# A two-layer encoder: the last 512 tokens split 384 and 128 instead of 256 and 256, a shorter final root, four final norms on GpSimd, and another order of the first loads

## The chip, the cores and the metric

One core of a Trainium2 chip runs the whole kernel. The metric is the device time of one execution in microseconds, the median of several. The engines are named as in the profile: PE is TensorE (PEld its weight loads), DVE is VectorE, ACT is ScalarE, POOL is GpSimd, SP is SyncE, which here only issues transfers. A small q (SPq, ACTq) stands for an engine's sequencer, which issues DMAs.

## The reference, cut to what matters

The input `x` is 1024 tokens by 1024 features in float32; two layers follow each other, and a last norm stands at the end. What the change touches is the first product of layer 0 and the end of layer 1:

```python
for l in range(DEPTH):                       # DEPTH = 2
    h = _rmsnorm(x, g_mix[l])                # x * rsqrt(mean(x*x) + 1e-6) * g
    p = h @ w_in[l]
    ...                                      # latent attention and a convolution branch
    x = x + y
    h2 = _rmsnorm(x, g_ffn[l])
    z = _dwconv(h2 @ w_up[l], w_dw_ffn[l], b_dw_ffn[l])
    zg, zv = jnp.split(z, 2, axis=-1)
    x = x + (jax.nn.silu(zg) * zv) @ w_down[l]
return _rmsnorm(x, g_final)
```

## The kernel before, in words

The residual stream lies transposed: eight blocks of 128 features (partitions) by 1024 tokens (columns). A product with float32 accuracy is made of three products of rounded operands: upper weight with upper x, upper with lower, lower with upper. So each operand is split in two on ACT (the rounded upper part) and DVE (the rest), and each product of a 128 x 128 weight tile with 512 tokens is three TensorE instructions.

**The start** is `run` (L367) and `first_sections` (L385). Three sections of the first weight matrix (g0, a0, g1) are multiplied with the eight blocks of x. The norm's gain is folded into x (`upper_x`, `lower_x`), and its root is applied later, to the products; for it ACT squares the blocks and DVE adds them up in `xss`. The work is written out by hand: the loads in program order on SP (one, of g0's first 256 columns, on ACT), then the casts and subtractions, then the products. TensorE begins with eleven products of ones (`WARM`), then six pairs on block 0 with g0 and a0, then `order` (L472): blocks 1 to 7 with all three sections, and g1 on blocks 0 and 1. The first 256 columns of a weight section are the tiles of blocks 0 and 1, the rest those of blocks 2 to 7. After block 5 the sums in `xss` are turned on TensorE (`turned`, 8 transposes), which needs the last addition.

**The end** is `down_steps` (L1196), the down projection, written as a list of steps: `steps[n]` holds the products of step n, and `put(n, rank, f)` places other work behind step n in order of rank. That fixes the order of the instructions on each engine; each still waits for its own data. In layer 1 the last six weight tiles (`TAIL_STEPS`) of the last product group are multiplied in eight steps: first for the token range `ENDS[0]`, feature blocks m = 0 to 3, then for `ENDS[1]`, 18 products a step. A finished piece is added to x on DVE (`evict_end`), squared on ACT, and the square is added to the sums on DVE (`gather_end`), but that of m = 3, which TensorE sums directly. `end_root` sums over features on TensorE (`column_sums`: an f32 product with a column of ones per 128 tokens, two passes each) and takes the inverse root on DVE (`roots`: nine small instructions). For `ENDS[0]` the root is spread back over features by transposes (`end_spread`), and `norm_apply` multiplies the blocks, on DVE out of PSUM, or on POOL for the blocks of `TAIL_POOL` with a copy that ACT makes, after ACT has multiplied the gain in (`end_scale`). SP stores each block, in the order of the program. For `ENDS[1]` the blocks, with their gains in, are turned on TensorE (`end_turn`), so that tokens lie on partitions and the root is one number per partition; `after` (L1358) multiplies by it, half on DVE, half on ACT, and stores to `out_tail`.

Of the kernel before, what the change touches and what calls it, by code (L numbers as in the profile page):

```python
# [16 lines left out]
T = 1024  # L17
# [14 lines left out]
EPS = 1e-6  # L32
RSQRT = 0x5F3759DF
GROUP = 2
SCALE = 1.0 / float(np.sqrt(NOPE + ROPE))
# [52 lines left out]
TAIL_STEPS = 6  # L88
ENDS = (slice(512, 768), slice(768, T))
LEAD_HEADS = 3  # L90
# [3 lines left out]
BANK_SET = {1: 0, 6: 0, 7: 0, 4: 0, 5: 1, 3: 1, 2: 1}  # L94
TAIL_POOL = (5, 7)
WARM = 11
# [20 lines left out]
class Encoder:  # L117
# [105 lines left out]

    def sumsq(self, acc, x, first, name, n=T, tag=None):
        nc = self.nc
        if first:
            nc.scalar.activation(out=acc, in_=x, func=AF.Square)
        else:
            sq = (self.tmp(tag, name) if tag else self.blk(name))[:, 0:n]
            nc.scalar.activation(out=sq, in_=x, func=AF.Square)  # L230
            nc.vector.tensor_tensor(out=acc, in0=acc, in1=sq, op=ALU.add)

    def column_sums(self, acc, name, parts, bank, more=None):
        nc = self.nc
        ps = bank(name + "p")
        blocks = [b for s in parts for b in range(s.start, s.stop, 128)]
        for i, b in enumerate(blocks):
            nc.tensor.matmul(ps[:, i:i + 1], acc[:, b:b + 128], self.ones[:, 0:1], start=more is None or i == 0, stop=more is None)
        for i in range(len(blocks) if more is not None else 0):
            nc.tensor.matmul(ps[:, i:i + 1], more[:, i * 128:(i + 1) * 128], self.ones[:, 0:1], start=False, stop=i == len(blocks) - 1)  # L240
        return ps[:, 0:len(blocks)]
# [10 lines left out]
    def roots(self, ps, w, n, name):  # L252
# [19 lines left out]
        return y  # L272

    def rsqrt_cols(self, acc, n, name, parts, bank, more=None, turned=False):
        w = sum(s.stop - s.start for s in parts) // 128
        if turned:
            return self.roots(self.turned(acc, name, parts, bank), w, n, name)
        return self.roots(self.column_sums(acc, name, parts, bank, more), w, n, name)

# [87 lines left out]
    def run(self):  # L367
        nc, a = self.nc, self.a
        self.par = [self.cp.tile([128, NPAR], F32, name="par0")]
        nc.sync.dma_start(out=self.par[0][:, 0:8], in_=a["par"][0][:, 0:8])  # L370
        self.x0 = self.blk("x0")
        nc.sync.dma_start(out=self.x0[:, HALVES[0]], in_=a["x"][0][:, HALVES[0]])
        self.ones = self.cp.tile([128, 128], F32, name="ones")
        nc.vector.memset(self.ones, 1.0)
        self.ones_r = self.cp.tile([128, 128], F32R, name="ones_r")
        self.xm = [self.dp.tile([8, 128, T], F32, name=f"x_mix{l}") for l in range(DEPTH)]
        self.actd = [self.dp.tile([NF, 128, T], F32, name=f"act{l}") for l in range(DEPTH)]
        self.wsd = [self.dp.tile([NF // 2, 2, 128, T], F32, name=f"ws{l}") for l in range(DEPTH)]
        self.xd = [a["x"], self.dp.tile([8, 128, T], F32, name="x_mid")]
        carry = None  # L380
        with self.tc.manual_schedule(engines=set(MANUAL)):
            for l in range(DEPTH):
                carry = self.layer(l, carry)

    def first_sections(self, l, supply):  # L385
# [3 lines left out]
             for n in names]  # L389
        x, acc = [self.x0] + [self.blk(f"x{k}") for k in range(1, 8)], self.blk(f"xss{l}")  # L390
        hl = [[self.tmp("m", f"xs{l}_{k}{i}", F32R) if k >= 4 else self.blk(f"xs{l}_{k}{i}", F32R) for i in "hl"]
# [24 lines left out]
        def upper_x(k, c=every):  # L416
            nc.scalar.activation(out=hl[k][0][:, c], in_=x[k][:, c], func=AF.Copy, scale=par[:, P_GMIX + k:P_GMIX + k + 1])

        def lower_x(k, c=every):
            nc.vector.scalar_tensor_tensor(out=hl[k][1][:, c], in0=x[k][:, c], scalar=par[:, P_GMIX + k:P_GMIX + k + 1],  # L420
                                           in1=hl[k][0][:, c].bitcast(F32), op0=ALU.mult, op1=ALU.subtract)

        def square(k):
            self.sumsq(acc, x[k], k == 0, f"xsq{l}_{k}")
# [11 lines left out]
        nc.sync.dma_start(out=self.par[0][:, 8:NPAR], in_=self.a["par"][0][:, 8:NPAR])  # L436
        self.par += [self.const(f"par{i}", [128, NPAR], self.a["par"][i]) for i in range(1, DEPTH)]
# [17 lines left out]
        lower(1, rest)  # L455
        lower_x(2)
        square(0)
        upper_x(3)
# [737 lines left out]
    def down_steps(self, l, steps, put):  # L1196
# [77 lines left out]
        def evict_end(c, m):  # L1274
            xm = x[4 + m][:, ENDS[c]]
            sub(xm, ps[BANK_SET[4], m][:, cols[c]], xm, ALU.add)

            sq[c, m] = self.blk(f"xsq{l}_e{c}{m}")[:, 0:256]
            nc.scalar.activation(out=sq[c, m], in_=xm, func=AF.Square)
# [46 lines left out]
        for m in range(4):  # L1326
# [3 lines left out]
            for c in range(2):  # L1330
                n = n5 + 4 * c + m
                put(n + 1 - c, 1 + c, lambda c=c, m=m: evict_end(c, m))
                if m < 3:
                    put(n + 1, 2.5 if c else 2.6, lambda c=c, m=m: gather_end(c, m))
        for f in range(NF):
# [22 lines left out]
        def after():  # L1358
            if not last:
                nxt["x"] = x  # L1360
                return nxt
            out = [self.blk(f"end{b}") for b in range(2)]
            for b in range(2):
                for i, cs in enumerate(HALVES):
                    o, ps, y = out[b][:, cs], turns[b, i], nxt["d"][:, b:b + 1]
                    if i == 0:
                        nc.vector.tensor_scalar(out=o, in0=ps, scalar1=y, scalar2=None, op0=ALU.mult)
                    else:
                        nc.scalar.activation(out=o, in_=ps, func=AF.Copy, scale=y)
                    (nc.scalar if b and i else nc.sync).dma_start(out=a["out_tail"][b][:, cs], in_=o)  # L1370

        def end_turn(i):
            for b, tag in enumerate(("d7", "d6") if i == 0 else ("d2", "d3")):
                turns[b, i] = self.pp.tile([128, 512], F32, name=f"end{i}{b}", tag=tag, bufs=1)
                at = ENDS[1].start + b * 128
                for k in range(4):
                    nc.tensor.transpose(turns[b, i][:, k * 128:(k + 1) * 128], x[4 * i + k][:, at:at + 128], self.ident)

# [5 lines left out]
        def end_root(c):  # L1384
            self.norm_root(l + 1, nxt, 1, spare, ENDS[c], sq.pop((c, 3)))

# [9 lines left out]
        if last:  # L1396
            put(n5 + 5, 0.5, lambda: end_root(0))
            put(n5 + 4, 3.5, lambda: end_scale(0))
            put(n5 + 6, 1.8, lambda: end_spread(0, (2, 5, 7, 0, 1)))
            put(n5 + 7, 3, lambda: end_apply(0, (3, 4, 6)))  # L1400
            put(n5 + 5, 3.5, lambda: end_scale(1, range(4)))
            for m in range(4):
                put(n5 + 4 + m, 2.55, lambda m=m: end_scale(1, (4 + m,)))
            put(n5 + 7, 3.9, lambda: end_turn(0))
            put(n5 + 7, 4, lambda: end_root(1))
            put(n5 + 7, 4.1, lambda: end_turn(1))
        return after

    def norm_sums(self, l, x, nxt, c, ks, cs=None):
# [3 lines left out]
        for k in ks:  # L1413
            self.sumsq(nxt["acc"][:, cs], x[k][:, cs], k == 0, f"xsq{l}_{cs.start}{k}", cs.stop - cs.start, None if c else "m")

# [399 lines left out]
def _layout(inputs):  # L1815
# [31 lines left out]
    def taps(w, k):  # L1847
# [4 lines left out]
         vec(f["g_conv_ln"]), vec(f["b_conv_ln"]), vec(f["g_ffn"]), taps(f["w_dw_ffn"], 3),  # L1852
         vec(f["b_dw_ffn"])], axis=2))
    out["g_final"] = c(f["g_final"].reshape(8, 128).T)
    out["ident"] = np.eye(128, dtype=np.float32)
# [22 lines left out]
```

## Time and profile before

| | us |
|---|---|
| median of 3 runs | 2251.2 (2250.36 to 2254.52) |
| the profiled execution | 2251.68 |
| its span | 2249.9 |
| PE busy in the span | 2225.7 |
| DVE, ACT, POOL busy | 1687.8, 1235.2, 693.4 |

The page gives busy time and its share of the span for each engine; PE is a pipelined engine, and its being busy does not say how much it computes. All durations below are from this one execution, so sums are made against 2251.68 and its span.

### The profile page before, as it was taken

To read this page: it belongs to the slowest core of one execution; us is meant where nothing else is said; L and a number is where in the kernel's file an instruction comes from. 1 tells how busy PE (TensorE), PEld (TensorE's weight loads), DVE (VectorE), ACT (ScalarE), POOL (GpSimd) and SP (SyncE) were. 2 spreads that over 40 slices of the span, in tenths; PEclk is the share of its full clock that TensorE was granted. 3 is DMA by queue.
4 is the path that set the end of the run, shared out by engine and by line. 5 is a ranking of instruction groups with operands and counts; after the bars stand their busy time and mean duration, and the time that the engine had idled before them with its cause. 6 is when DMAs were issued, how large, how long until landed. Compare 5 with 4: busy or idle time off the path is not lost. (4 is left out here: it accounts for less than half of the span.)

```text
span 2249.9 us, 34444 instructions
## 1 busy us (share of the span) xinstructions
PE 2225.7 (99%) x12746; PEld 1790.3 (80%) x12746; DVE 1687.8 (75%) x2241; ACT 1235.2 (55%) x1885; POOL 693.4 (31%) x781
## 2 busy tenths in 40 slices
PE   9999999999999999999999999999999999999998
PEld 7887666888888888888888876668888888888887
DVE  6998898669777776776559778876787777768765
ACT  5444777447655555544523457774475555555444
POOL 1221586332333332002412226652323333320032
PEclk9999999999999999999999999999999999999999
DMA  6889998765999998935968999986669999988356
GB/s 186 162 171 279 193 216 184 206 174 125 227 269 304 276 300 206 331 106 144 207 133 167 201 265 198 196 197 177 159 155 232 291 291 278 292 211 300 102 127 168
DMA packets 201160, 472.85 MB, mean 210 GB/s; under 512 B 28352, under 2 KB 35616, under 8 KB 200992
## 3 DMA queue, kind: packets, MB, share of 16 engines
q0 software_dynamic: 102704, 220.91, 48.9%
q1 hardware_dynamic: 98000, 249.35, 33.6%
q8 instruction: 100, 1.64, 0.3%
q14 instruction: 68, 0.56, 0.1%
q10 hardware_dynamic: 288, 0.39, 0.0%
HBM read 306.14 MB, written 80.40 MB: 172 GB/s over the span
## 5 line engine op out<-in xcount | busy, mean ns | idle before, releaser
L1078 PE MATMUL p<-b,w 128*128 128x512 f32 x3552 | 808.1, 389 | 0.2
L1078 PEld LDWEIGHTS p<-b,w 128*128 128x128 f32 x3552 | 665.9, 188 | 141.8 <-DVE w L1456 1.7
L1266 PE MATMUL pd<-ab,wd 128*128 128x512 f32 (+1 forms) x1920 | 422.3, 381 | 0.0
L1266 PEld LDWEIGHTS pd<-ab,wd 128*128 128x128 f32 x1920 | 350.8, 188 | 69.4 <-DVE ab L1456 0.4
L181 POOL DMA_DIRECT2D w<-wu x96 | 84.4, 879 | 358.9 <-ACT w L180 323.8
L1520 DVE TENSOR_REDUCE mx<-s 128x1 f32<-128x1024 f32 x128 | 156.2, 1220 | 37.1 <-PE s L1518 28.7
L1528 ACT ACTIVATE p<-s,mx 128x1024 f32<-128x1024 f32 x128 | 142.8, 1116 | 59.2 <-DVE mx L1520 57.3
L1468 DVE SCALAR_TENSOR_TENSOR o<-zg,par,o 128x1023 f32<-128x1023 f32 x88 | 112.8, 1283 | 76.7 <-ACT o L1462 75.3
L181 POOL DMA_DIRECT2D w<-in_w_up x116 | 100.5, 867 | 200.2 <-ACT w L180 179.0
L1719 DVE SCALAR_TENSOR_TENSOR conv<-gate,par,conv 128x1009 f32<-128x1009 f32 (+7 forms) x112 | 142.3, 1274 | 3.6 <-ACT conv L577 1.0
L180 ACT ACTIVATE w<-w 128x512 fp32r<-128x512 f32 x212 | 133.5, 630 | 3.0
L1454 ACT CAST ab<-ac 128x512 fp32r<-128x512 f32 x130 | 80.1, 617 | 97.7 <-DVE ac L1201 95.5
L1027 DVE TENSOR_TENSOR zg<-p,zg 128x512 f32<-128x512 f32 x88 | 60.5, 690 | 97.0 <-PE p L1078 90.3
L1567 PE MATMUL o<-pt,v 128*64 128x256 f32 x1024 | 126.8, 386 | 2.8 <-DVE yt L1581 1.6
L852 POOL DMA_DIRECT2D wd<-in_w_down x44 | 32.4, 738 | 308.5 <-PE pd L1266 165.2
L1468 DVE SCALAR_TENSOR_TENSOR v<-zv,par,v 128x1023 f32<-128x1023 f32 x88 | 112.4, 1279 | 10.5 <-ACT v L1462 10.4
L1454 ACT CAST w<-wu 128x512 fp32r<-128x512 f32 x84 | 51.8, 619 | 123.9 <-DVE wu L1027 121.3
L1541 PEld LDWEIGHTS t<-ident,p 64*128 64x128 f32 x2048 | 77.9, 138 | 41.1 <-issue 27.1
L1045 ACT CAST w<-wu 128x512 fp32r<-128x512 f32 x96 | 58.9, 614 | 92.9 <-DVE wu L1027 89.2
L1567 PEld LDWEIGHTS o<-pt,v 128*64 128x64 f32 x1024 | 67.9, 136 | 52.5 <-issue 18.5
L1544 DVE COPY pt<-t 128x512 f32<-128x512 f32 x128 | 87.5, 683 | 28.0 <-PE t L1541 26.8
L1738 POOL DMA_DIRECT2D conv<-late x75 | 68.3, 924 | 123.6 <-DVE late L1732 54.3
(2142 smaller groups left out, 4396.0 us busy)
## 6 DMA issues: line engine op xcount, KB each, us to landing
w<-in_w_up POOLq DMA_DIRECT2D x232, 256.0 KB, 7.4
wu<-in_w_up SPq DMA_DIRECT2D x88, 512.0 KB, 5.6
w<-wu POOLq DMA_DIRECT2D x96, 256.0 KB, 5.8
sd<-in_w_down SPq DMA_DIRECT2D x44, 512.0 KB, 9.8
ws<-sd SPq DMA_DIRECT2D x44, 512.0 KB, 6.9
wd<-in_w_down POOLq DMA_DIRECT2D x88, 256.0 KB, 5.3
act<-v SPq DMA_DIRECT2D x36, 512.0 KB, 5.7
ac<-act SPq DMA_DIRECT2D x72, 256.0 KB, 6.1
```

The lines of the kernel that those rows point to most:

```text
L180: self.nc.scalar.activation(out=lo, in_=hi.bitcast(F32), func=AF.Copy, scale=-1.0)
L181: self.nc.gpsimd.dma_start(out=lo, in_=src, accum_op=ALU.add)
L1078: nc.tensor.matmul(ps, w[p][:, k * 128:(k + 1) * 128], b[:, q], start=(i in (1, 5, 2) and k == 0 and t == 0), stop=(k == 3 and t == 2), sk ...
L1266: nc.tensor.matmul(ps[t, m][:, cs], w[i, j][p][:, m * 128:(m + 1) * 128], b[:, q, cs], start=(i in (1, 5, 2) and j == 0 and s == 0), stop= ...
L1454: nc.scalar.copy(out=t[:, 0], in_=src)
L1468: self.nc.vector.scalar_tensor_tensor(out=o[:, a:b], in0=z[:, at + a:at + b], scalar=self.par[l][:, tap:tap + 1], in1=o[:, a:b], op0=ALU.m ...
L1520: nc.vector.tensor_reduce(out=mx, in_=ps, op=ALU.max, axis=AX.X, negate=True)
L1528: nc.scalar.activation(out=p, in_=ps, func=AF.Exp, bias=mx, accum_out=st["sums"][:, qt:qt + 1])
L1541: nc.tensor.transpose(t[:, i, qi, :], st["p"][2 * qp + qi][r, ks], self.ident[r, r])
L1544: nc.vector.tensor_copy(out=pt[:, :, :, 1, :], in_=tp[1])
L1567: nc.tensor.matmul(po[ROW_TILES[i % 2], cs], v[k // 2][:, k % 2, h * 64:h * 64 + 64], pt[:, i, :], start=k < 2, stop=k > 5)
L1719: self.nc.vector.scalar_tensor_tensor(out=y[:, lo:hi], in0=u[:, lo + s:hi + s], scalar=self.tap(l, j, t), in1=y[:, lo:hi], op0=ALU.mult, o ...
```

## The change

The range of the last 512 tokens is split 384 and 128. The output in turned form thus has 128 tokens (`out_tail` is 128 by 1024), and is written in two pieces of 256 features for each half. The sums of the second part are no longer added up on DVE: TensorE sums the accumulated blocks and four squares directly. The final root uses seven instructions; the epsilon is added earlier, in the accumulation. POOL multiplies four blocks (4, 5, 6, 7) of the first part instead of two. At the start the gains are laid in one tensor with the first 512 tokens of block 0 (`head`), which ACT's queue loads together with half of x0 and half of x1; the first columns of all three weight sections are loaded first on SP, and all three are used on block 0 before block 1.

```diff
-ENDS = (slice(512, 768), slice(768, T))
+ENDS = (slice(512, 896), slice(896, T))
-TAIL_POOL = (5, 7)
+TAIL_POOL = (4, 5, 6, 7)
...
+    def final_roots(self, ps, w, name):
...
+        nc.vector.tensor_scalar(out=y.bitcast(I32), in0=ps.bitcast(I32), scalar1=-0.5, scalar2=float(RSQRT), op0=ALU.mult, op1=ALU.add)
+        nc.vector.tensor_tensor(out=t, in0=y, in1=y, op=ALU.mult)
+        nc.vector.scalar_tensor_tensor(out=t, in0=t, scalar=s, in1=ps, op0=ALU.mult, op1=ALU.mult)
+        nc.vector.scalar_tensor_tensor(out=v, in0=t, scalar=a, in1=t, op0=ALU.add, op1=ALU.mult)
+        nc.vector.scalar_tensor_tensor(out=t, in0=t, scalar=c, in1=t, op0=ALU.add, op1=ALU.mult)
+        nc.vector.scalar_tensor_tensor(out=y, in0=v, scalar=b, in1=y, op0=ALU.add, op1=ALU.mult)
+        nc.vector.scalar_tensor_tensor(out=y, in0=t, scalar=d, in1=y, op0=ALU.add, op1=ALU.mult)
...
-        nc.sync.dma_start(out=self.par[0][:, 0:8], in_=a["par"][0][:, 0:8])
-        self.x0 = self.blk("x0")
-        nc.sync.dma_start(out=self.x0[:, HALVES[0]], in_=a["x"][0][:, HALVES[0]])
+        self.head = self.blk("head")[:, 0:520]
+        nc.scalar.dma_start(out=self.head, in_=a["head"])
...
-        nc.scalar.dma_start(out=w[0][0][:, some], in_=self.weight_source(l, names[0])[:, some])
+        for k, c in ((0, right), (1, left)):
+            nc.scalar.dma_start(out=x[k][:, c], in_=self.xd[0][k][:, c])
...
-        load_x(0, right)
+        load(0, some)
         load(1, some)
-        load_x(1)
-        load(2, every)
+        load(2, some)
+        load_x(1, right)
         load(0, rest)
         load(1, rest)
+        load(2, rest)
         for k in range(2, 8):
             load_x(k)
...
-        upper_x(1)
-        lower_x(1)
-        cast(2, every)
-        lower(2, every)
+        cast(2, some, True)
+        lower(2, some)
+        for c in HALVES:
+            upper_x(1, c)
+            lower_x(1, c)
...
         lower_x(2)
+        cast(2, rest)
+        lower(2, rest)
         square(0)
...
-        order = [(1, 0), (1, 1)] + [(k, 2) for k in range(2)] + [(k, i) for k in range(2, 8) for i in range(3)]
+        order = [(0, 2), (1, 0), (1, 1), (1, 2)] + [(k, i) for k in range(2, 8) for i in range(3)]
...
+                if (c, m) == (1, 1):
+                    steps.append(lambda: ([product(4, j, (1,), cols[1]) for j in range(tail, tail + 2)], end_root(0),
+                                          [product(4, j, (1,), cols[1]) for j in range(tail + 2, half)]))
+                    continue
...
-            self.norm_root(l + 1, nxt, 1, spare, ENDS[c], sq.pop((c, 3)))
+            self.norm_root(l + 1, nxt, 1, spare, ENDS[c], [sq.pop((c, m)) for m in range(0 if c else 3, 4)])
...
+            out, y = self.blk("end"), nxt["d"]
+            for part in (slice(0, 256), slice(256, 512)):
+                o = [out[:, HALVES[i]][:, part] for i in range(2)]
+                nc.vector.tensor_scalar(out=o[0], in0=turns[0][:, part], scalar1=y, scalar2=None, op0=ALU.mult)
+                nc.scalar.activation(out=o[1], in_=turns[1][:, part], func=AF.Copy, scale=y)
+                for i, queue in enumerate((nc.sync, nc.scalar)):
+                    queue.dma_start(out=a["out_tail"][:, HALVES[i]][:, part], in_=o[i])
+            end_apply(0, (3,))
...
+            put(n5 + 6, 3, lambda: end_spread(0, (4, 0, 1, 5)))
+            put(n5 + 7, 3, lambda: end_apply(0, (2, 6)))
...
-            put(n5 + 7, 4.1, lambda: end_turn(1))
+            put(n5 + 7, 4.1, lambda: (end_turn(1), end_apply(0, (7,))))
```

## Rows read from the trace of the kernel before

**Rows 1.** The page, part 1: busy time, share of the span, instructions.
```profile
PE 2225.7 (99%) x12746; PEld 1790.3 (80%) x12746; DVE 1687.8 (75%) x2241; ACT 1235.2 (55%) x1885; POOL 693.4 (31%) x781
```

**Rows 2.** Order of time, start: start, duration, engine, line, operation, idle before.
```profile
0.74 0.40 ACTq L396 DMA_DIRECT2D wg00r<-in_w_in  x1
...
1.05 4.77 PEld L399 LDWEIGHTS warm<-ones 128*128 128x128 f32 x22 [1.05 <-DVE ones L374]
...
1.18 0.42 SPq L372 DMA_DIRECT2D x<-in_x  x1
...
11.39 0.30 PEld L515 LDWEIGHTS pg<-xs_1l,wg00h 128*128 128x128 f32 x2 [1.02 <-DVE xs_1l L420]
...
12.10 0.84 ACT L410 CAST wa00h<-wa00r 128x768 fp32r<-128x768 f32 x1
...
13.38 1.15 ACT L417 ACTIVATE xs_2h<-x,par 128x1024 fp32r<-128x1024 f32 x1 [0.45 <-DMA x<-in_x]
...
14.57 1.28 DVE L420 SCALAR_TENSOR_TENSOR xs_2l<-x,par,xs_2h 128x1024 fp32r<-128x1024 f32 x1 [0.36 <-ACT xs_2h L417]
...
16.56 1.28 DVE L420 SCALAR_TENSOR_TENSOR xs_3l<-x,par,xs_3h 128x1024 fp32r<-128x1024 f32 x1 [0.71 <-ACT xs_3h L417]
16.75 0.41 PEld L515 LDWEIGHTS pg<-xs_2l,wg00h 128*128 128x128 f32 x2
...
27.09 3.88 DVE L231 TENSOR_TENSOR xss<-xss,xsq 128x1024 f32<-128x1024 f32 x3
...
32.62 1.02 PEld L248 LDWEIGHTS rx0t<-ident,xss 128*128 128x128 f32 x8
```

**Rows 3.** Windows, start: stretch, us, busy of each engine, PEclk, DMA share, GB/s.
```profile
5.00:13.00 8.00, 6.86 (x27) 4.65 (x26) 5.12 (x7) 5.37 (x7) 0.00 (x0) 1.00 0.98 358
```

**Rows 4.** Chain of waits, end: start, duration, what.
```profile
2199.92 11.79 PE pd L1266 x52
...
2234.65 0.45 PE rx_512p L240 x4
...
2237.78 2.16 PE pd L1266 x18
...
2239.97 0.43 DVE x L1201
...
2242.31 0.14 DVE rx_768v L263
...
2244.05 0.75 DVE end L1367
```

**Rows 5.** Order of time, SP alone, end.
```profile
2244.82 1.49 SPq L1370 DMA_DIRECT2D out_tail<-end  x3
```

**Rows 6.** DMA issues, 0 to 14 us: what, count, size, us to landing.
```profile
x<-in_x SPq DMA_DIRECT2D x2, 256.0 KB, 3.6
```

**Rows 7.** Order of time, end.
```profile
2214.83 1.66 ACT L230 ACTIVATE xsq<-x 128x512 f32<-128x512 f32 x3
...
2239.70 0.35 ACT L1427 COPY rx<-ry_512s 128x256 f32<-128x256 f32 x1
...
2242.00 0.94 PEld L1377 LDWEIGHTS end<-ident,x 128*128 128x128 f32 x8
```

**Rows 8.** Chain of waits, in the attention of layer 1.
```profile
1329.00 0.65 PE t L1541 x16
```

**Rows 9.** Groups by form, 2226 to 2251 us: busy us, mean ns, idle before.
```profile
L1201 DVE TENSOR_TENSOR x<-pd,x 128x256 f32<-128x256 f32 x8 | 3.3, 418 | 0.4 <-PE pd L1266 0.4
...
L1445 POOL TENSOR_TENSOR x<-x,rx 128x256 f32<-128x256 f32 x2 | 1.6, 812 | 24.6 <-ACT rx L1427 24.6
...
L1367 DVE TENSOR_SCALAR end<-end,rx_768y 128x512 f32<-128x512 f32 x2 | 1.4, 748 | 0.0
```

**Rows 10.** DMA issues, 2236 to 2251 us: what, count, size, us to landing.
```profile
out_y<-x SPq DMA_DIRECT2D x8, 128.0 KB, 1.8
out_tail<-end SPq DMA_DIRECT2D x3, 256.0 KB, 3.0
```

More of the change, by code (lines that the diff above doesn't have):

```diff
@@ L33 @@
 RSQRT = 0x5F3759DF
+QUARTIC = (1.7208752561885539, (-1.5547911482404086, 5.05455810860835), (-7.29998737667443, 15.593052263180018))
 GROUP = 2
@@ L222, in tiled, with sumsq @@
         return lambda k: (hi[:, k * n:(k + 1) * n], lo[:, k * n:(k + 1) * n])
-    def sumsq(self, acc, x, first, name, n=T, tag=None):
+    def sumsq(self, acc, x, first, name, n=T, tag=None, guard=None):
         nc = self.nc
@@ L230, in sumsq @@
             nc.scalar.activation(out=sq, in_=x, func=AF.Square)
+            if guard:
+                nc.vector.scalar_tensor_tensor(out=acc, in0=acc, scalar=guard, in1=sq, op0=ALU.add, op1=ALU.add)
+                return
             nc.vector.tensor_tensor(out=acc, in0=acc, in1=sq, op=ALU.add)
@@ L238, in column_sums @@
             nc.tensor.matmul(ps[:, i:i + 1], acc[:, b:b + 128], self.ones[:, 0:1], start=more is None or i == 0, stop=more is None)
-        for i in range(len(blocks) if more is not None else 0):
-            nc.tensor.matmul(ps[:, i:i + 1], more[:, i * 128:(i + 1) * 128], self.ones[:, 0:1], start=False, stop=i == len(blocks) - 1)
+        for e, sq in enumerate(more or ()):
+            for i in range(len(blocks)):
+                nc.tensor.matmul(ps[:, i:i + 1], sq[:, i * 128:(i + 1) * 128], self.ones[:, 0:1], start=False,
+                                 stop=e == len(more) - 1 and i == len(blocks) - 1)
         return ps[:, 0:len(blocks)]
@@ L272, in roots @@
         return y
+    def final_roots(self, ps, w, name):
+        nc = self.nc
+        v, y, t = (self.cp.tile([128, 8], F32, name=name + e, tag="rs" + e, bufs=2)[:, 0:w] for e in "vyt")
+        s, (a, b), (c, d) = QUARTIC
+        nc.vector.tensor_scalar(out=y.bitcast(I32), in0=ps.bitcast(I32), scalar1=-0.5, scalar2=float(RSQRT), op0=ALU.mult, op1=ALU.add)
[5 more added lines that the diff above has]
+        nc.vector.scalar_tensor_tensor(out=y, in0=t, scalar=d, in1=y, op0=ALU.add, op1=ALU.mult)
+        return y
     def rsqrt_cols(self, acc, n, name, parts, bank, more=None, turned=False):
@@ L277, in rsqrt_cols @@
             return self.roots(self.turned(acc, name, parts, bank), w, n, name)
+        if more:
+            return self.final_roots(self.column_sums(acc, name, parts, bank, more), w, name)
         return self.roots(self.column_sums(acc, name, parts, bank, more), w, n, name)
@@ L389, in first_sections, with tokens @@
              for n in names]
-        x, acc = [self.x0] + [self.blk(f"x{k}") for k in range(1, 8)], self.blk(f"xss{l}")
+        x, acc = [self.blk(f"x{k}") for k in range(8)], self.blk(f"xss{l}")
+        gains = self.head[:, 0:8]
+        def tokens(k, c):
+            return self.head[:, 8:520] if k == 0 and c == HALVES[0] else x[k][:, c]
         hl = [[self.tmp("m", f"xs{l}_{k}{i}", F32R) if k >= 4 else self.blk(f"xs{l}_{k}{i}", F32R) for i in "hl"]
@@ L446, in first_sections @@
         lower(1, some)
-        upper_x(1)
-        lower_x(1)
-        cast(2, every)
-        lower(2, every)
+        cast(2, some, True)
+        lower(2, some)
+        for c in HALVES:
+            upper_x(1, c)
+            lower_x(1, c)
         cast(0, rest)
@@ L1276, in evict_end @@
             sub(xm, ps[BANK_SET[4], m][:, cols[c]], xm, ALU.add)
-            sq[c, m] = self.blk(f"xsq{l}_e{c}{m}")[:, 0:256]
+            sq[c, m] = self.blk(f"xsq{l}_e{c}{m}")[:, 0:ENDS[c].stop - ENDS[c].start]
             nc.scalar.activation(out=sq[c, m], in_=xm, func=AF.Square)
@@ L1331, in down_steps @@
                 n = n5 + 4 * c + m
-                put(n + 1 - c, 1 + c, lambda c=c, m=m: evict_end(c, m))
-                if m < 3:
-                    put(n + 1, 2.5 if c else 2.6, lambda c=c, m=m: gather_end(c, m))
+                put(n + 1 - c, (0.4 if m == 3 else 1) + c * 1, lambda c=c, m=m: evict_end(c, m))
+                if m < 3 and c == 0:
+                    put(n + 1, 2.6, lambda c=c, m=m: gather_end(c, m))
         for f in range(NF):
@@ L1361, in after @@
                 return nxt
[L1362 to L1370, printed above, removed]
-        def end_turn(i):
[L1373 to L1377, printed above, removed]
+            out, y = self.blk("end"), nxt["d"]
[6 more added lines that the diff above has]
+            end_apply(0, (3,))
+        def end_turn(i):
+            turns[i] = self.pp.tile([128, 512], F32, name=f"end{i}", tag="d2" if i else "d7", bufs=1)
+            for k in range(4):
+                nc.tensor.transpose(turns[i][:, k * 128:(k + 1) * 128], x[4 * i + k][:, ENDS[1]], self.ident)
         def end_scale(c, ks=TAIL_POOL):
@@ L1413, in norm_sums @@
         for k in ks:
-            self.sumsq(nxt["acc"][:, cs], x[k][:, cs], k == 0, f"xsq{l}_{cs.start}{k}", cs.stop - cs.start, None if c else "m")
+            self.sumsq(nxt["acc"][:, cs], x[k][:, cs], k == 0, f"xsq{l}_{cs.start}{k}", cs.stop - cs.start, None if c else "m",
+                       EPS * D / 128 if (l, c, k) == (DEPTH, 1, 3) else None)
     def norm_root(self, l, nxt, c, bank, cs=None, more=None):
@@ L1870 @@
     aps["out"] = nc.dram_tensor("out_y", (8, 128, T), F32, kind="ExternalOutput").ap()
-    aps["out_tail"] = nc.dram_tensor("out_tail", (2, 128, D), F32, kind="ExternalOutput").ap()
+    aps["out_tail"] = nc.dram_tensor("out_tail", (128, D), F32, kind="ExternalOutput").ap()
     with tile.TileContext(nc) as tc:
@@ L1875 @@
     y = np.asarray(r.results[0]["out_y"]).reshape(D, T)
-    tail = np.asarray(r.results[0]["out_tail"]).reshape(256, D)
-    return np.concatenate([y.T[:T - 256], tail])[None]
+    tail = np.asarray(r.results[0]["out_tail"])
+    return np.concatenate([y.T[:T - 128], tail])[None]
```

22 lines of the change are left out of this document (12 added, 10 removed).

## The prediction

> **What bounds the kernel now.** The page's first part comes first: TensorE is busy for 99% of the span [rows 1], so a change can pay only where TensorE waits, or by the work that it gets. The edits touch the first 33 us and the last 30; between them the instructions are the same, so I read only the two ends: by windows, in order of time, then the chain of waits.
>
> *Start.* Eleven warm-up products keep TensorE in work from 1.05 to 5.82 [rows 2]. The window from 5 to 13 us then holds 6.86 us of TensorE work in 8.00, with the DMA engines at 0.98 [rows 3]. From 11.39 products follow each other; the weight load of 11.39 shows the last wait, 1.02 us for xs_1l [rows 2]. Block x2 is next: it lands at 13.38, its upper part is made from there, its lower part from 14.57 for 1.28 us, so until 15.85, and TensorE takes it at 16.75, 0.9 us after it is ready. The next knot is at 32.62, where the sums of squares are turned: VectorE's additions end at 27.09 + 3.88 = 30.97 [rows 2].
>
> *End.* The chain of waits is TensorE products until 2239.95; from there VectorE has it: the last eviction at 2239.97, the final root from 2242.31 to 2244.05, then the output block [rows 4]. SP begins three output issues at 2244.82 that take 1.49 us [rows 5]; the last thus starts near 2245.9, and the span ends at 2249.9: 9.95 us from the last product to the end.
>
> **The change part by part: the start.** The first x and the gains go to ACT's queue, issued at 0.74, where before x was issued on SP at 1.18 [rows 2] and landed 3.6 us later [rows 6], at 4.78. They land some 0.4 us sooner. That is worth nothing: the first real product follows the warm-up, whose count stays, at 5.82. Without that cover it would give 0.4.
>
> Before, 12 products of the first list and 2 more run between 5.82 and 11.39: 14 at 0.2267 (11.79 us for 52 [rows 4]) are 3.2 us, so 2.4 us are waiting. After, a0's first columns come second on SP, x1 comes in halves on both queues, and six products of g1 on x0 stand ahead of x1's. I cost these waits at zero after. What is late next is x2: 36 products precede it in both orders, so without waits TensorE would take xs_2h at 5.82 + 36 x 0.2267 = 13.98 and ask for xs_2l at 14.43. Before, xs_2l is ready at 15.85, 2.47 after x2's landing. x2's issue moves from ninth to eighth on SP, and an issue takes about 0.44; the bytes ahead of it stay the same and the DMA engines are nearly full [rows 3], so I take 0.4 us sooner. Bounds: 0 (the bytes decide) and 0.9 (two queues fill the engines sooner). Then TensorE takes xs_2l at 15.5 in place of 16.75: -1.25.
>
> A part comes back at the sums. ScalarE now has, between xs_2h and xs_3h, a cast of 768 columns (0.84 [rows 2]) and a square in two halves (1.1, from 1.66 for three of 512 [rows 7]) in place of one of 1024 (about 1.0). xs_3h comes 0.9 - 0.4 = 0.5 later, and VectorE, which has run without a gap since xs_3l at 16.56 [rows 2], ends its additions at 31.5; TensorE is there at 31.4. Cost 0.1. **Start: -1.1**, bounds -1.8 and 0. The gains that now come in x's rows, the later load of the whole parameter block, and ACT's two further issues lie under the warm-up: 0.
>
> **The end: products.** The step list runs 72 products on the first part and 72 on the second. Now these are 256 columns at 2.16/18 = 0.120 [rows 4]. At 384 columns, halfway to 512 (0.2267), 0.173: 72 x 0.053 = +3.8. For 128 columns no row of this kind of product exists. Below: the line through the two, 0.067. Above: the warm-up's 128-column products, 4.77/22 = 0.217 [rows 2]. Nearest rows: transposes of 128 columns by 128 take 0.94 for eight [rows 7], and the column sums move one column and still take 0.45 for four [rows 4], 0.112: the weight load alone sets that. I take 0.110: 72 x -0.010 = -0.7. By bounds: -3.8 and +7.0.
>
> The Trainium skill bears on this (TensorE: Matmul & The Clock Gate, Back-to-back issue gap): a stream of weight load and 128-column matmul settles near 81 ns each. By that figure the 72 would be 2.1 us cheaper than by mine. In this trace only the attention's transposes reach it, 0.65 for 16 on two row groups, 0.081 per group [rows 8]; the full-array rows do not.
>
> The first root sums one accumulated block row and one square of three 128-blocks: 12 passes for 8 (+0.45), and its spread has 6 transposes for 4 (+0.2). The sums stand after six of the second block's products and wait for a square whose products ended 24 products earlier: no stall. Last product: 3.8 - 0.7 + 0.65 = **+3.75**, at 2243.7.
>
> **The end: after the last product.** To the root, 2.36 us before: eviction, two additions on VectorE, and three applies between. After, the gathers of the second part are gone; TensorE has 4 transposes (0.45), 10 sum passes (1.13) and a handover (0.15): 1.72, while eviction and square of 128 columns run beside it. -0.64. The root has 7 instructions for 9 at 0.193 (1.74/9 [rows 4]): -0.39. The output: from root to last issue 1.85 before; after, two pieces of 256 columns on VectorE at 0.42 and block 3's apply of 384 at 0.58 (between 0.42 for 256 and 0.75 for 512 [rows 9]) and a wait, 1.47: -0.38. From last issue to the end 4.0 before, with transfers of 256 KB at 3.0 [rows 10]; after, 192 KB with fewer ahead; 128 KB took 1.8 [rows 10]. I take 2.2 + 1.0: -0.8 (bounds -1.2 and 0). Sum **-2.2**.
>
> **GpSimd and SP.** Four applies of 384 columns on GpSimd, at 0.81 for 256 [rows 9] 1.22 each, 4.9 us. They start after the spread, one step of 18 products ahead of the last product: 2241.7, plus ACT's copy (0.35 for 256 [rows 7], so 0.5, and 0.2 of handover): 2242.4 to 2247.3. SP issues in program order, and block 7 stands ahead of the output pieces: the first piece, ready at 2243.7 + 1.72 + 1.35 + 0.42 = 2247.2, is issued behind it, the last issue slips by about 0.2. VectorE in return loses two applies, which lay beside products: 0. **End: 3.75 - 2.2 + 0.2 = +1.75.**
>
> Sum: -1.1 + 1.75 = +0.65. The profiled execution took 2251.68 (span 2249.9 and 1.8 around it), 0.5 above the median of 2251.2. Forecast: 2251.2 + 0.6 = **2251.8**, no change that can be measured: 0.2% (4.5 us) is about what a measurement of this kernel can tell.
>
> **Rivals.**
> *A. Narrow products are cheap (0.18).* If the weight load hides, 0.081 per product as in the attention rows, the last product comes 2.1 sooner. Against: the one-column sums at 0.112. The gain doesn't arrive whole: GpSimd's chain moves only with the 54 products before the spread, by 1.6, to 2245.7, and then SP holds the output pieces behind block 7; the last issue comes at 2247.0, the end about 1.5 sooner than forecast: 2250.3; at 0.067 about 2249.6. The Trainium skill's 81 ns, above, is the figure of this rival.
> *B. Narrow products cost twice (0.08): slower.* The 128-column products keep the pace of the warm-up's, 0.217. 72 x 0.107 = +7.7: 2259.5. For it: that row is the only plain product of this width. Against: its operands are plain f32 in two passes, and it ran before TensorE had done anything else; a 128-column transpose takes half of it later. It makes the kernel measurably slower from 0.165 on (0.11 + 3.9/72).
> *C. GpSimd's four applies set the end (0.08).* VectorE works beside them all the time; at 1.6 each in place of 1.22 the chain ends 1.5 later and the output pieces with it: 2253.3. For it: SP's order. Against: the 812 ns row was taken beside a busy VectorE too. The Trainium skill (GPSIMD Engine Reference, Key points) says that GpSimd shares its SBUF interfaces with VectorE and contends with instructions of two SBUF inputs. By that, the row of 812 ns has such slowing in it already; no row here shows more.
> *D. The start changes nothing (0.12).* x2 lands no sooner, since more rows are of 1 and 2 KB, and the waits only move from x0's weights to x2: 2252.9. With the upper bound in place of that, x2 0.9 sooner: 2251.3.
>
> **How the numbers follow.** My case 0.54, A 0.18, D 0.12, B 0.08, C 0.08. From 2248.5 (A with the start's best bound, and the last transfer's) to 2255.0 (C, D and the last transfer at its dear bound together) all but B is covered. Faster by 0.2% needs -4.5, only A with every bound on its good side: 0.04. Slower: B and a piece of C: 0.10. Same: 0.86.
>
> **What would show it.** Right: first real product still at 5.8; xs_2l taken near 15.5; the transposes of the sums near 31.4 with a wait of some 0.1; 384-column products at 0.17 and 128-column ones at 0.11; last product 3 to 4 us later in the span's end part, root of 7 instructions in 1.35, end 7.8 after the last product; SP's first output piece right behind block 7. Wrong: 128 columns at 0.07 to 0.08 (A) or 0.2 (B), GpSimd at 1.6 (C), xs_2l at 15.9 or later (D).

## The result, and the profile after

The changed kernel takes 2256.98 us against 2251.6 for the kernel before beside it: ratio 1.0024 [1.0018, 1.0031], slower by 5.4 us (4.1 to 7.0). This is the median of 17 runs; an eighteenth, at a granted clock of 0.266, took 8022.84 us and is left out (with it the median is 2257.39). The forecast was 2251.8 with a range up to 2255.0. It was wrong, on the side of rival B.

The profiled execution took 2254.1 (span 2252.3), so it is one of the quicker ones of this kernel. I therefore compare stages, not spans: the start, and the stretch from the transposes `rx_0t`, from which on the work of the end begins, to the last instruction. That stretch took 38.19 us before (2211.71 to 2249.9) and 46.03 after (2206.27 to 2252.3): +7.84, where +1.75 was forecast. The start gained 1.8, where 1.1 was forecast. Together +6.0, close to the measured 5.4; the rest of the profiled execution, the same instructions in both, happened to run 3.6 us quicker, as the spread between runs allows.

The page's first part answers to [rows 1]: as many matmuls, 7.7 us more of them.
```profile
PE 2233.4 (99%) x12746; PEld 1800.7 (80%) x12746; DVE 1684.4 (75%) x2235; ACT 1237.1 (55%) x1889; POOL 696.1 (31%) x783
```

The chain of waits through the end (start, duration, what; compare [rows 4]):
```profile
2206.27 0.44 PE rx_0t L254 x4
2206.71 5.49 PE pd L1300 x24
2212.20 0.44 PE rx_0s L307 x4
2212.63 17.89 PE pd L1300 x108
2230.52 0.61 PE rx_512p L242 x6
2231.13 0.67 PE rx_512p L245 x6
2231.80 6.36 PE pd L1300 x30
2238.16 0.66 PE rx_512s L307 x3
2238.82 0.64 PE ry_512s L307 x3
2239.46 3.73 PE pd L1300 x18
2243.20 0.87 PE end L1412 x4
2244.07 0.22 PE rx_896p L242 x2
2244.29 1.72 PE rx_896p L245 x8
...
2246.03 0.17 DVE rx_896y L284
...
2247.07 0.17 DVE rx_896y L290
```
The reader is to see two paces in it. The 108 products up to 2230.52 hold 12 of 512 columns, 72 of 384 and the first 24 of 128. Twelve at 0.2267 are 2.72, 24 at 0.11 are 2.64, and that leaves 0.174 for one of 384 columns: as forecast. Behind the column sums the same 128-column products take 6.36/30 and 3.73/18, both 0.21; the six transposes of the spread 0.22 in place of 0.11; the last ten passes 1.94 together. Everything TensorE does from there is twice as dear.

The windows say why (stretch, us, busy of PE, PEld, DVE, ACT and POOL, PEclk, DMA share, GB/s):
```profile
2228.00:2230.00 2.00, 2.00 (x20) 2.00 (x20) 0.60 (x2) 0.62 (x2) 0.00 (x0) 1.00 0.00 0
2230.00:2232.00 2.00, 2.00 (x20) 2.00 (x19) 0.34 (x2) 1.76 (x6) 0.00 (x0) 0.96 0.00 0
2232.00:2234.00 2.00, 2.00 (x11) 2.00 (x10) 0.88 (x7) 0.63 (x3) 0.00 (x0) 0.50 0.00 0
...
2240.00:2242.00 2.00, 2.00 (x11) 2.00 (x11) 0.00 (x1) 0.00 (x0) 1.94 (x3) 0.50 0.59 210
```
The granted clock goes from 1.00 to 0.50 (2.4 to 1.2 GHz) at about 2231.8, just behind the twelve column-sum passes, and stays there to the end. TensorE and its weight load are busy for the whole of each window, before and after: this is no fall after idling.

The start, in order of time (start, duration, engine, line, operation, idle before), against [rows 2]:
```profile
5.22 3.72 SPq L432 DMA_DIRECT2D x<-in_x  x6
5.71 0.33 PEld L504 LDWEIGHTS pg<-xs_0h,wg00h 128*128 128x128 f32 x1
11.84 1.15 ACT L443 ACTIVATE xs_2h<-x,head 128x1024 fp32r<-128x1024 f32 x1 [1.42 <-DMA x<-in_x]
14.96 0.41 PEld L549 LDWEIGHTS pg<-xs_2l,wg00h 128*128 128x128 f32 x2
30.82 1.02 PEld L254 LDWEIGHTS rx0t<-ident,xss 128*128 128x128 f32 x8
```
The first real product stands where it stood. Block x2 lands at 11.84 in place of 13.38, TensorE takes its lower part at 14.96 in place of 16.75, and the 1.8 us are still there at 30.82 (32.62 before). The landing of x2 alone did not give them: its lower part was ready at 14.32 (13.03 + 1.29, second list below), 0.6 before TensorE came for it, and before the change it was ready ahead of TensorE too (15.85 for 16.75). TensorE comes sooner because waits ahead of x2 are gone. Before, weight loads waited 0.79 and 0.35 us (first list, from the trace of before) and 1.02 at 11.39 [rows 2]; after, the last such wait is one of 0.49 at 7.11. At 15.85 x2 would then have held TensorE up; its early landing let the gain through.
```profile
8.04 0.30 PEld L470 LDWEIGHTS pa<-xs_0h,wa00h 128*128 128x128 f32 x2 [0.79 <-ACT wa00h L410]
...
10.07 0.30 PEld L515 LDWEIGHTS pg<-xs_1h,wg00h 128*128 128x128 f32 x2 [0.35 <-ACT xs_1h L417]
```
```profile
13.03 1.29 DVE L446 SCALAR_TENSOR_TENSOR xs_2l<-x,head,xs_2h 128x1024 fp32r<-128x1024 f32 x1 [1.57 <-ACT xs_2h L443]
```

### The profile page after: what moved, and what is told of

The parts are those of the page before. It is cut to its first block, busy times and chain, and to the rows that moved or that the text cites. A ratio compares the mean times of both kernels' runs of the same rounds, so it can differ in the third digit from the quotient of the medians.

```text
span 2252.3 us, 34445 instructions
## 1 busy us (share of the span) xinstructions
PE 2233.4 (99%) x12746; PEld 1800.7 (80%) x12746; DVE 1684.4 (75%) x2235; ACT 1237.1 (55%) x1889; POOL 696.1 (31%) x783
## 5 line engine op out<-in xcount | busy, mean ns | idle before, releaser
L1300 PE MATMUL pd<-ab,wd 128*128 128x512 f32 (+2 forms) x1920 | 429.7, 386 | 0.0
L1300 PEld LDWEIGHTS pd<-ab,wd 128*128 128x128 f32 x1920 | 358.8, 191 | 69.0
L1492 DVE TENSOR_TENSOR ab<-ac,ab 128x512 fp32r<-128x512 f32 x130 | 89.3, 689 | 22.7 <-ACT ab L1490 15.7
```

The costliest lines, as they stand in the source:

```text
L1300: nc.tensor.matmul(ps[t, m][:, cs], w[i, j][p][:, m * 128:(m + 1) * 128], b[:, q, cs], start=(i in (1, 5, 2) and j == 0 and s == 0), stop= ...
```

## The experiments

All do the whole computation. Each is set against runs of the kernel before on its own chip.

**The two ends apart.** The start's edits alone, put on the kernel before:
```diff
-        nc.sync.dma_start(out=self.x0[:, HALVES[0]], in_=a["x"][0][:, HALVES[0]])
+        nc.scalar.dma_start(out=self.head, in_=a["head"])
...
-        order = [(1, 0), (1, 1)] + [(k, 2) for k in range(2)] + [(k, i) for k in range(2, 8) for i in range(3)]
+        order = [(0, 2), (1, 0), (1, 1), (1, 2)] + [(k, i) for k in range(2, 8) for i in range(3)]
```


> The start edits alone, the end as before. Theory (the whole loss is in the end, the start gains): block x2 is taken 1.8 us sooner in the trace of the change (xs_2l at 14.96 in place of 16.75, the turned sums at 30.82 in place of 32.62), so this kernel is 1.8 us faster than before: 2249.8 beside 2251.6, the granted clock 1.00 in every part of the end. Rival (the start's gain is eaten by waits in the attention): no difference, 2251.6 within 0.5.


Measured: 2250.89 against 2251.55, 0.9993 [0.9984, 1.0002]. The interval (-3.6 to +0.4) holds the expected gain of 1.8 and, at its edge, none; the time alone does not show the gain. Its trace shows the gain where the change's does: x2 landed at 11.78, the turned sums at 30.94.

The end's edits alone:
```diff
-ENDS = (slice(512, 768), slice(768, T))
+ENDS = (slice(512, 896), slice(896, T))
-TAIL_POOL = (5, 7)
+TAIL_POOL = (4, 5, 6, 7)
...
+    def final_roots(self, ps, w, name):
```


> The end edits alone, the start as before. Theory (the granted clock falls to half while 128-column products run): the end is 7.8 us longer, as in the trace of the change, 2259.4 beside 2251.6; the clock falls to 0.50 some 4 us after the first 128-column product. Rival (the clock falls only together with something that the start does): clock 1.00, products of 128 columns at 0.10, and the end 1.8 us longer: 2253.4.


Measured: 2260.7, 1.0034 [1.0021, 1.0046]. The whole loss is in the end, and the clock falls at the same place: 1.00 until the twelve passes (2237.35 to 2238.63), 0.50 from then on.

**Is it the width of the products?** The change, with the second part's products over 256 columns again (128 of them a second time, added to sums that have been read by then); everything else of the end stays:
```diff
+        wide = [cols[0], slice(256, 512)]
-                steps.append(lambda c=c, m=m: [product(4, j, (m,), cols[c]) for j in range(tail, half)])
+                steps.append(lambda c=c, m=m: [product(4, j, (m,), wide[c]) for j in range(tail, half)])
```


> The changed kernel, but the products of the last 128 tokens are run over 256 columns; the extra 128 columns go over finished, already evicted sums and are read by nobody. More work for TensorE. Theory (narrow products let the clock fall): the clock stays at 1.00, the 72 products take 0.12 each (8.6 us in place of 12.5), transposes and sums behind them take half: 6 us faster than the change, 2251.4 beside 2257.4. Rival 1 (the column sums and transposes between the products, not their width, let it fall): clock 0.50 again, products at 0.21 or more, 2258 or more. Rival 2 (a narrow product is slow as such): 2253, with the clock at 0.50 all the same in the transposes.


Measured: 2253.86, 1.0009 [1.0, 1.0018]. The clock stays at 1.00, and products with *more* columns end sooner (a window, then the chain):
```profile
2234.00:2236.00 2.00, 2.00 (x18) 2.00 (x18) 1.33 (x8) 0.93 (x4) 0.00 (x0) 1.00 0.00 0
```
```profile
2234.03 3.69 PE pd L1300 x30
...
2238.38 2.15 PE pd L1300 x18
```
0.12 each, against 0.21 for half the columns in the change. From `rx_0t` (2208.34) to the last instruction (2249.1) the end takes 40.8 us, 5.3 less than in the change; 6 were expected.

The kernel before, with each 256-column product of the second part made into two of 128:
```diff
-                steps.append(lambda c=c, m=m: [product(4, j, (m,), cols[c]) for j in range(tail, half)])
+                steps.append(lambda c=c, m=m: [product(4, j, (m,), s) for j in range(tail, half)
+                                               for s in ((cols[0],), (slice(256, 384), slice(384, 512)))[c]])
```


> The kernel before, but each 256-column product of its second part is two of 128 columns (same weights loaded twice); sums, transposes and everything else as before. Theory (narrow products let the clock fall): clock 0.50 after some 4 us of them, then 0.21 each; 36 at 0.10 and 108 at 0.21 in place of 72 at 0.12, and the work behind them at half: about 19 us slower, 2271. Rival (sums and transposes in between let it fall): clock 1.00, 144 at 0.10 in place of 72 at 0.12: 5.8 us slower, 2257.4.


Measured: 2267.42, 1.0066 [1.0053, 1.008]. Narrow products bring the low clock to the old root, split and GpSimd share too; there are only eight passes here (2237.56 to 2238.40), and the clock fell some 2.5 us behind them, among narrow products (0.94 in the window 2240 to 2241, 0.50 in the next).

**Or the one-column passes among them?** The kernel above, with the first part's root and its spread moved behind all products, so that 144 narrow products stand alone (one execution):
```diff
-            put(n5 + 5, 0.5, lambda: end_root(0))
+            put(n5 + 7, 2.2, lambda: end_root(0))
-            put(n5 + 6, 1.8, lambda: end_spread(0, (2, 5, 7, 0, 1)))
+            put(n5 + 7, 2.3, lambda: end_spread(0, (2, 5, 7, 0, 1)))
```


> As e4 (the kernel before with two 128-column products for each of 256 in the second part), but the root and spread of the first part come behind all products, so that 144 narrow products run without anything between them. In e4 they ran 8.4 us at 1.00, and the clock fell 3 to 4 us after the column sums that followed. Theory W (narrow products alone let the clock fall, only later than I thought): it falls to 0.50 inside the 144 products (14.4 us at 0.10). Theory W+S (it takes the column sums, which move one column per pass, on top of the narrow products): 1.00 until the last product, and it falls only in or behind the sums that now come after them.


Measured: 2262.38. All products ran at the full clock; it fell only behind the sums, and in this kernel TensorE also waits there:
```profile
2244.00:2246.00 2.00, 2.00 (x20) 2.00 (x20) 0.00 (x0) 0.00 (x0) 0.00 (x0) 1.00 0.00 0
2246.00:2248.00 2.00, 1.06 (x10) 0.97 (x9) 1.19 (x6) 0.42 (x1) 0.00 (x0) 1.00 0.00 0
2248.00:2250.00 2.00, 1.03 (x5) 1.06 (x6) 1.02 (x6) 0.00 (x0) 0.00 (x0) 0.66 0.00 0
```
So 128 columns alone do not lower the clock: sixteen microseconds of them didn't.

The opposite: the kernel before, its products untouched, with the eight passes of the first part's sums made five times over (the same sums, so 40 passes; one execution):
```diff
+        for _ in range(5 if more is not None and parts[0].start == 512 else 1):
+            for i, b in enumerate(blocks):
...
```


> The kernel before with its 256-column products, but the column sums of the first part are run five times over (40 passes of one column in place of 8, some 4.5 us). Theory W+S read as 'few columns per us, whoever moves them': the clock falls to 0.50 during or soon behind the sums, the rest of the products takes 0.21 each, 36 x 0.09 = 3.3 us on top of the 3.6 us of sums. Theory W (only narrow products of long standing): clock stays at 1.00 and the kernel is 3.6 us slower.


Measured: 2257.32. Chain of waits, then windows:
```profile
2235.79 0.46 PE rx_512p L241 x4
2236.26 0.85 PE rx_512p L239 x4
...
2239.67 3.75 PE pd L1267 x18
```
```profile
2235.00:2236.00 1.00, 1.00 (x12) 1.00 (x11) 0.00 (x0) 0.00 (x0) 0.00 (x0) 1.00 0.00 0
2236.00:2237.00 1.00, 1.00 (x8) 1.00 (x7) 0.00 (x0) 0.00 (x0) 0.00 (x0) 0.54 0.00 0
2242.00:2243.00 1.00, 1.00 (x7) 1.00 (x6) 0.11 (x1) 0.97 (x3) 0.00 (x0) 0.54 0.00 0
2243.00:2244.00 1.00, 1.00 (x11) 1.00 (x10) 0.32 (x1) 1.00 (x4) 0.00 (x0) 1.00 0.00 0
```
The passes began at 2233.67; the clock fell in the middle of them, while TensorE was busy without a gap. It came back, near 2242.9, behind 256-column products; in the change, behind 128-column ones, it never did. Of the 18 products of 256 columns (3.75 in all), those at half clock follow each other every 0.213 by their starts, and the last three, at 1.00 again, every 0.12 or so. At half clock that is the same as 128 columns in the change, and as one column (0.85/4). At 0.50 none of these forms is cheaper than another.

**The test of the cause.** The change as it is, 128-column products included; only the sums of the last two roots move 128 columns of ones in place of one, and the root reads the first of each 128:
```diff
+        n = 128 if more is not None else 1
-            nc.tensor.matmul(ps[:, i:i + 1], acc[:, b:b + 128], self.ones[:, 0:1], start=more is None or i == 0, stop=more is None)
+            nc.tensor.matmul(at(i), acc[:, b:b + 128], self.ones[:, 0:n], start=more is None or i == 0, stop=more is None)
```


> The changed kernel, but each pass of the column sums of the last two roots multiplies with 128 columns of ones in place of one; the same sum then stands in 128 columns, and the root reads the first. No pass is added or moved. By e5, 144 narrow products run at 1.00; by e6, column sums alone bring the clock down. Theory (the one-column passes let the clock fall, and 128-column products cannot lift it again): with 128 columns in every pass the clock stays at 1.00, 48 products come back from 0.21 to 0.10 and the passes behind from 0.21 to 0.11, -5 and -1.1: 6 us faster than the change, 2251.4 beside 2257.4. Rival (it is the f32 passes, whatever they move, or the long stretch of narrow work): clock 0.50 again from about 2232, and no faster than the change.


Measured: 2252.94, 1.0005 [0.9996, 1.0014], an interval that does not touch the change's [1.0018, 1.0031]. More work on TensorE and some 4 us less time: 1.9 above its runs of before, where the change is 5.4 above its own. The timed runs show the clock too: its mean over a run is 0.995 to 0.997 in the 17 of the change, 0.998 to 1.0 in the twelve of this kernel. Windows and chain:
```profile
2232.00:2234.00 2.00, 2.00 (x21) 2.00 (x19) 1.19 (x8) 1.25 (x5) 0.00 (x0) 1.00 0.00 0
...
2238.00:2240.00 2.00, 2.00 (x21) 2.00 (x20) 0.81 (x2) 0.71 (x2) 2.00 (x3) 1.00 0.68 241
```
```profile
2232.52 3.30 PE pd L1302 x30
...
2236.49 1.96 PE pd L1302 x18
...
2240.07 0.17 DVE rx_896y L286
...
2240.26 1.02 DVE rx_896t L287
```
The clock holds, the narrow products take 0.11, and the end from `rx_0t` (2206.88) to the last instruction (2247.2) is 40.3 us: +2.1 against before, where the forecast had +1.75. With the start's -1.8 that makes +0.3; the interval of the timed runs, -0.9 to +3.2, holds it. That the one-column passes among narrow products brought the clock down is shown. With the clock kept, the forecast's sum for the end comes out, but not term by term: the last product comes 3.3 later than before (31.57 for 28.24 behind `rx_0t`; forecast +3.75), and what follows it gives back 1.2 (8.74 for 9.95), where -2.2 + 0.2 = -2.0 was forecast; the difference is the wait described next. That the two errors partly cancel is luck.

**A wait that the forecast had not.** In the last fence the root's second instruction takes 1.02 us instead of 0.17; it took 0.98 with the wide second part, too. GpSimd's four applies ran there at the time. That kernel again, with all applies on VectorE (one execution):
```diff
-TAIL_POOL = (4, 5, 6, 7)
+TAIL_POOL = ()
...
-            put(n5 + 7, 3, lambda: end_apply(0, (2, 6)))
+            put(n5 + 7, 3, lambda: end_apply(0, (2, 6, 7)))
```


> As e3 (the second part's products over 256 columns, clock at 1.00), but the four applies of the first part that GpSimd has run on VectorE. In e3 the second instruction of the final root, a product of two inputs on one column, took 0.97 us and ended when GpSimd's last apply ended. Theory (VectorE's two-input instruction waits while GpSimd works on the shared memory port): it takes 0.16 here, and the root 1.35 in all in place of 2.0. Rival (a slow read behind TensorE's transposes): 0.97 again.


Measured: 2253.7, no shorter as a whole, since the applies then stand ahead of the root on VectorE (`x L1484 x3`, 1.57 us on the chain). But the instruction is back at its size. With GpSimd (order of time on GpSimd, then the chain):
```profile
2239.28 3.88 POOL L1482 TENSOR_TENSOR x<-x,rx 128x384 f32<-128x384 f32 x4 [27.52 <-ACT rx L1464]
```
```profile
2242.22 0.98 DVE rx_896t L285
```
Without (chain):
```profile
2245.83 0.17 DVE rx_896t L285
```
GpSimd's last apply ends at 2239.28 + 3.88 = 2243.16, the held instruction at 2243.20. In the change itself the low clock hid this: its root began at 2246.03, after GpSimd had ended (2243.95). The trace of before had such a row already, in its chain: VectorE's last addition of two inputs, beside GpSimd's first apply (from 2240.13), took 0.73 where the one at 2239.12 took 0.42.
```profile
2240.41 0.73 DVE xss L1201
```

**Whose is the start's gain?** The start's edits, with the first tokens and the two halves on SP ahead of the weights instead of on ACT's queue (one execution):
```diff
-        nc.scalar.dma_start(out=self.head, in_=a["head"])
+        nc.sync.dma_start(out=self.head, in_=a["head"])
-            nc.scalar.dma_start(out=x[k][:, c], in_=self.xd[0][k][:, c])
+            nc.sync.dma_start(out=x[k][:, c], in_=self.xd[0][k][:, c])
```


> The start edits alone (as e1), but the first x with the gains, the other half of x0 and half of x1 go on SP's queue with all the rest, ahead of the weights. In the changed kernel x2 landed at 11.84, 1.5 us sooner than before, where I had 0.4. Theory (a second queue fills the DMA engines sooner): here x2 lands at 13.0 to 13.4 again. Rival (the order and the sizes of the loads did it): 11.8 to 12.3.


Measured: 2251.26. Block x2 landed at 13.11 (before 13.38, two queues 11.78), the turned sums at 31.57. Windows from 4 to 8 us, first the kernel before, then the change, then one queue:
```profile
4.00:6.00 2.00, 2.00 (x11) 2.00 (x10) 0.70 (x2) 1.16 (x2) 0.00 (x0) 1.00 0.73 238
6.00:8.00 2.00, 1.49 (x5) 0.58 (x4) 1.34 (x3) 0.57 (x2) 0.00 (x0) 1.00 0.99 294
```
```profile
4.00:6.00 2.00, 2.00 (x11) 2.00 (x10) 1.04 (x2) 1.17 (x2) 0.00 (x0) 1.00 1.02 336
6.00:8.00 2.00, 1.94 (x8) 1.09 (x8) 1.66 (x5) 1.58 (x4) 0.00 (x0) 1.00 1.02 390
```
```profile
4.00:6.00 2.00, 1.56 (x10) 1.37 (x9) 0.00 (x0) 0.93 (x2) 0.00 (x0) 1.00 0.96 297
6.00:8.00 2.00, 1.34 (x4) 0.76 (x5) 1.95 (x5) 1.03 (x2) 0.00 (x0) 1.00 0.78 284
```
The second queue is worth 1.3 us of x2's landing and 0.6 of the 1.7 at the turned sums (32.62, 31.57, 30.94); the rest is the new order of loads and products. From 4 to 8 us the change moves 1.45 MB (2 us each at 336 and 390 GB/s), the others 1.06 and 1.16. That is the time of the three issues taken off SP: its first weight block is issued at 0.74 with two queues, at 2.12 with one, 1.38 later. TensorE loses its 0.6 there and not at x2: with one queue its first real product waits 0.93 us for that block and begins at 6.49 in place of 5.77. The Trainium skill (DMA: Bandwidth & Descriptors, "Issuing engines are not separate DMA queues") says that issuing from several engines saves only the time to issue, usually small beside the transfer. These runs agree on what is saved; here, where the first transfers wait for their issues, it is the gain.

**The part worth keeping.** The kernel before with the start's edits and the seven-instruction root, the split left at 256 and 256 and GpSimd at two blocks:
```diff
+        if more:
+            return self.final_roots(self.column_sums(acc, name, parts, bank, more), w, name)
```


> The start edits and the root of seven instructions, with the kernel before's 256 and 256 split, its eviction order and its two GpSimd applies. If the loss is all in the narrow second part, this keeps the gains: -1.8 at the start, two instructions of 0.193 off the final root: 2.2 us faster than before, 2249.4 beside 2251.6, clock 1.00. Rival (start gain does not reach the end, as e1's 0.7 may hint): 0.4 to 1.0 faster.


Measured: 2250.37 against 2251.29, 0.9993 [0.9984, 1.0001]. The lowest ratio of all versions, shared with the start's edits alone, and not told from the kernel before: the expected gain of 2.2 lies inside the interval (-3.6 to +0.2), as does none.

## Why the prediction was wrong, point by point

**The step that failed** is the term "I take 0.110: 72 x -0.010 = -0.7" for the narrow products, with the 128-column transposes and the passes behind them. The size 0.110 was right for TensorE at full clock (0.110 and 0.109 with the wide sums). It silently carried the clock of 1.00 from the stretch of wider products into one of 128-column products and one-column passes, where nothing in the trace of before shows it. The clock fell to 0.50 behind the twelve one-column passes, and 48 of the 72 products cost 0.21. The term by what it measured, against the same stage of before:

| from `rx_0t` to the end | forecast | measured |
|---|---|---|
| 72 products of 384 columns | +3.8 | +3.6 (0.174 each) |
| 72 products of 128 columns | -0.7 | +3.8 (24 at 0.11, 48 at 0.21) |
| sums and spread of the first root | +0.65 | +1.35 (spread 1.30 for 0.44) |
| last product | +3.75 | +8.7 (28.24 to 36.93) |
| after the last product | -2.2 | -0.85 (9.95 to 9.1) |

The 256-column products of before average 0.1244 over the whole stage ((38.19 - 9.95) less the other pieces of that chain), not the 0.120 of the last 18; I set the measured column against that. The -0.85 is the clock too: four transposes and ten passes took 2.81, at 0.112 each they are 1.57; without these 1.24 us it is -2.1, against the forecast's -2.2 and its +0.2 for SP.

*Rival B* had the side and nearly the number (2259.5), for a reason that fell: it took 0.217 from the warm-up as the price of the form, for all 72. The form costs 0.11, and plain f32 is hardly dearer: the twelve wide passes of the test of the cause took 1.39, 0.116 each. The row of the warm-up is a row at half clock. The trace of before has no record of the granted clock ahead of 6.32, and the windows print 1.00 where there is none; so its speed is to be read from the instructions. In the run with one queue the records begin at 4.83, and there the starts of the same passes go from 0.213 us apart to 0.111. Their sum, before and then with one queue:
```profile
1.06 5.06 PE L399 MATMUL warm<-ones 128*128 128x128 f32 x22 [1.06 <-DVE ones L374]
```
```profile
1.06 4.51 PE L404 MATMUL warm<-ones 128*128 128x128 f32 x22 [1.06 <-DVE ones L373]
```
So 0.217 was what 128 columns cost at half clock, and 48 of the 72 paid it. That B's total came near is partly luck: it charged 72 products, and nothing for the transposes and passes that were dear as well.

*Rival A* is out: no run shows a full-array 128-column product below 0.109, so the 81 ns that the Trainium skill (TensorE: Matmul & The Clock Gate, Back-to-back issue gap) gives did not come about here.

*Rival C* is out in its own form, and GpSimd was quicker than forecast: 3.88/4 = 0.97 for 384 columns, not 1.22. The row of 0.81 for 256 columns, scaled up, was too dear. The prediction looked for contention in GpSimd's rows alone ("no row here shows more"); VectorE's row of 0.73, above, shows it. What the four applies do cost is another thing, 0.8 us of VectorE's root wherever the clock holds. The rule of the Trainium skill that the prediction weighed there is told more exactly in SBUF — State Buffer ("SBUF: two separate sides"): a VectorE instruction with two SBUF inputs and a GpSimd instruction that reads SBUF exclude each other for the whole of the one that came first. The held instruction, freed 0.04 us after GpSimd's last one, agrees; the one-input instruction just ahead of it took its usual 0.17.

*The start* (-1.1; D: nothing). Better than forecast, and x2 was wrong in it. I made x2 what TensorE waits for after the change, and moved it by its place among SP's issues, 0.4 us. In fact its issue comes later, at 5.22 in place of 4.50, and it lands 1.54 sooner, because the transfers ahead of it began sooner and filled the DMA engines from 4 us on. The bound for that, 0.9, was too tight, and with x2 so early TensorE did not wait for it at all. The gain is the waits for a0's weights and for x1, which the forecast had put at zero after the change and which are gone; x2 only let it through. The loss of 0.1 at the turned sums did not appear: VectorE's additions ended at 30.26 (26.38 + 3.88), ahead of TensorE. D is out.

*What held*: the first real product (5.71), 384 columns at 0.174 (0.173), the root of seven instructions (2246.03 to 2247.24, 1.2 for 1.35), SP's output pieces behind block 7, though only in order: block 7 was done at 2243.95, the first piece was issued at 2247.77, and the 0.2 forecast for it did not arise.

**What stays open.** Which amount of narrow work lowers the clock: twelve passes among narrow products did it at once, eight did it 2.5 us later, eight or twelve among 256-column products did not, 40 did. These runs don't give a rule, and the document draws none. Whether 320 and 192 columns would hold the clock was not tried. An uneven split has a price without the clock, too: a pair of products costs 0.284 (0.174 + 0.110) in place of 0.249, 2.5 us over the 72, and what comes after the last product gave 1.2 back (9.95 to 8.74 with the wide sums).

## What to carry to other kernels

The price of a TensorE instruction is read with the granted clock beside it, and where the trace has no record of the clock, as in the first microseconds here, by comparing the row with the same instruction elsewhere. A change that makes a stretch of work narrower can take that clock away while the engine stays 100% busy: a forecast for narrow products needs a rival "at half clock" whose price is doubled, and the first thing to look at afterwards is PEclk by windows, not busy time. If it has fallen among tiny matmuls, giving these more columns can keep it: here that cost 0.11 us (1.39 for 1.28). And a block's landing in the first microseconds follows when all transfers ahead of it were issued, more than its own place in a queue.

## What the runs showed of the hardware that I had not expected

- A granted clock of 0.50 with TensorE and its weight load busy 2.00 of 2.00 us, for 14 us, behind one-column passes (the change, and the end alone); 144 products of 128 columns by themselves kept 1.00.
- At 0.50, one column, 128 and 256 columns all cost 0.21 us; at 1.00, one and 128 columns 0.11, 256 columns 0.12, 384 0.174. The warm-up's passes went at the slow pace, 0.213, until 4.83 in the run with one queue.
- Twelve passes with 128 times the columns took 1.39 us (0.72 + 0.67) against 1.28 with one, and saved some 4 us behind them.
- A one-column, two-input VectorE instruction lasted 0.98 us beside a GpSimd apply and 0.17 without.
